# The first two key tiles of an attention stage, their penalties and the first query are loaded by another route

## The chip, the cores and the metric

The kernel runs on one core of a Trainium2 chip, as one launch. The metric is the device time of an execution in microseconds (us); of several executions the median is taken.

The core has five engines with instruction queues of their own: TensorE (PE, with its weight loads as PEld), VectorE (DVE), ScalarE (ACT), GpSimd (POOL) and SyncE (SP). In this kernel SP issues all the transfers (DMA) between the memory off the core and the core's own.

## The reference, cut to what matters

One layer of an encoder for 2048 prompt frames and 8 x 16 sample frames. A wide input projection feeds two mixers: a gated one over 128-frame chunks, and a sparse attention, in which an indexer scores all earlier keys for each query and only the best 256 take part. Their outputs are merged, projected and normed.

```python
def _sparse_attend(q, qi, wi, q_pos, k, v, kidx, k_pos, topk):
    rel = relu(einsum('bqhd,bld->bqhl', qi, kidx) * IDX_DIM ** -0.5)
    score = einsum('bqhl,bqh->bql', rel, wi) * N_IDX_HEADS ** -0.5
    score = where(chunk_mask(q_pos, k_pos), score, -inf)
    top_val, top_idx = lax.top_k(score, topk)          # 256 of up to 2048 keys
    k_sel, v_sel = k[top_idx], v[top_idx]
    logits = einsum('bqhgd,bqnhd->bqhgn', qg, k_sel) * HEAD_DIM ** -0.5
    p = softmax(where(top_val > -inf, logits, -inf))
    return einsum('bqhgn,bqnhd->bqhgd', p, v_sel)
```

## The kernel before

Rows (frames) are handled in tiles of 128: tiles 0 to 15 are the prompt, tile 16 the samples. There are three parts.

**Projections and selection.** `phase_p1` and `phase_p2` make the projections for one half of the tiles at a time. Each product is made from three matmuls of a high and a low part (`mm3`, line 175), after `split_hi` on ACT (line 181) and `split_lo` on DVE or POOL (line 184). Between these matmuls the generator `select` is woven in, once per tile, on two lanes. It makes the scores of a tile (`scores`: the indexer's query is loaded into a buffer tagged `qi`, split into `qih` and `qi`, and multiplied with the indexer's keys, lines 544 and 545), then finds the 256th largest score bit by bit, counting in turn on DVE (line 623) and on ACT (line 633). At the end it turns the scores into a penalty per key, in pieces of 512 columns: a scan on DVE (line 669) into a buffer `pre` (tag `r`, three buffers), a compare on DVE (line 674) into the buffer `pen` (one buffer), a scaling on ACT (line 675), and a store to the scratch tensor `pen_s` (line 676). All 256 first keys are chosen for tiles 0 and 1, so `select_all_of` writes their penalties at the start of the program (lines 685 to 687). The last tiles are 15 on one lane and 14 on the other.

**Attention.** `phase_b` runs over the prompt's tiles from 0 to 15. For each it loads keys, values, penalties and queries. `load_kv` transposes the key tile on PE (line 724), splits it into `kst` (ACT and DVE), and splits the values into `vst` (ACT and POOL). `attend_logits` makes the logits (lines 767 and 768), subtracts the penalties and takes the maximum on DVE (line 769), and takes the exponential on ACT (line 774). `attend_values` transposes the results (line 791) and multiplies them with the values (line 808). The samples' attention and the first merges are woven in behind.

**Merge and output**, `phase_c`.

Between the first and the second part stands `load_first` (before). It loads the key tiles 0 and 1 into buffers tagged `r`, the penalty of tile 0 into the buffer tagged `pen`, and the query of tile 0 into the indexer's buffer `qi`, which it splits into `qih` and `qi` at once. All these buffers lie in the pool `tk`, which stays open. The pool `bp` of the attention takes the room of the projections' weights.

```python
    back = weave(phase_p2(0, hT), back, 0.95)
    drain(back)
    load_first()
    wp.close()
    hp.close()
    bank.set(mm=3, tr=3, po=1, ix=1)
    bp = Pool("bp")
```

The instructions of each engine are put into a fixed order by a scheduler, which works on its own estimate of times when the program is built; each engine then works its list off from the first to the last. So a change in one place may reorder instructions in others.

## Time and profile before

| | |
|---|---|
| device time, median of 3 runs | 2202.66 us (2201.59 to 2203.26) |
| profiled execution: its own time | 2199.08 us |
| profiled execution: span from first to last instruction | 2197.3 us |
| PE busy | 2117.8 us (96%) |
| DVE busy | 1534.8 us (70%) |
| ACT busy | 1271.4 us (58%) |
| POOL busy | 588.1 us (27%) |
| mean granted TensorE clock | 0.988 of full speed |

The span is the time between the first and the last instruction of the one execution that was profiled; its own device time is 1.78 us longer. Busy time of PE is modelled from pipelined matmuls, so 96% means that it rarely stood still, not that it worked at its peak.

### The profile page before, as it was taken

The numbers are of one execution on the slowest core, as the hardware profiler recorded it, in microseconds if no ns is written. First come the engines' busy times: TensorE is split into PE (matmuls) and PEld (weight loads), VectorE is DVE, ScalarE is ACT, GpSimd is POOL, SyncE is SP. The second block draws the span as 40 slices with busy tenths as digits, with TensorE's granted clock in tenths as the row PEclk, the third lists the DMA queues.
The fourth block names the chain that finished last, engine by engine and source line by source line (L and its number), as shares of the span: only waits on it lengthen the run. The fifth ranks groups of instructions, "written<-read, shape, count | busy, mean of one in ns | idle before, by whom it ended". The sixth has DMA issues, their size and how long they took to land.

```text
span 2197.3 us, 38208 instructions
## 1 busy us (share of the span) xinstructions
PE 2117.8 (96%) x13896; PEld 2008.8 (91%) x13896; DVE 1534.8 (70%) x3926; ACT 1271.4 (58%) x2280; POOL 588.1 (27%) x693
## 2 busy tenths in 40 slices
PE   8999999999999999999999999599999999999998
PEld 7999999999999988999999999588889998987886
DVE  7128777988887847778865785587867788855443
ACT  6237666567766644556764665487766667743221
POOL 1222132222242222223252221232254433233000
PEclk9999999999999999999999999799999999999999
DMA  6234243122252323222233222454254431054342
GB/s 205 88 105 131 63 119 101 50 77 83 71 153 87 95 76 120 59 61 63 67 116 102 63 83 74 114 145 103 59 169 132 121 104 40 11 161 155 130 153 77
DMA packets 251005, 218.83 MB, mean 100 GB/s; under 512 B 46528, under 2 KB 238656, under 8 KB 250816
## 3 DMA queue, kind: packets, MB, share of 16 engines
q1 hardware_dynamic: 250816, 216.39, 33.5%
q8 instruction: 109, 1.79, 0.3%
q14 instruction: 80, 0.66, 0.1%
HBM read 152.45 MB, written 63.81 MB: 98 GB/s over the span
## 4 chain that ended last, share of the span: by engine, by line
PE 80%; DMA 6%; DVE 5%; ACT 4%; issue 2%; POOL 1%; SPq 1%; ACTq 0%; DVEq 0%; POOLq 0%
PE ps_mm L175 54%; PE ps_po L808 5%; PE ps_tr L791 5%; PE ps_mm L767 3%; PE ps_ix L544 2%; PE ps_ix L545 2%; PE ps_mm L768 2%; PE ps_ix L175 2%; DMA ws<-in_w_in_dram 2%; DMA q<-q_s 1%; POOL wl L184 1%; PE ps_mm L819 1%; DMA x<-in_x_prompt_dram 1%; DVE junk L623 1%; PE ps_tr L439 1%
## 5 line engine op out<-in xcount | busy, mean ns | idle before, releaser
L184 POOL TENSOR_TENSOR wl<-ws,wh 128x256 fp32r<-128x256 f32 (+1 forms) x376 | 300.7, 831 | 912.1 <-ACT wh L181 841.1
L175 PE MATMUL ps_mm<-wh,hh 128*128 128x256 f32 (+1 forms) x1360 | 390.4, 288 | 6.4 <-ACT hh L181 3.7
L175 PE MATMUL ps_mm<-wh,hl 128*128 128x256 f32 (+1 forms) x1360 | 392.0, 289 | 0.9 <-DVE hl L184 0.9
L175 PE MATMUL ps_mm<-wl,hh 128*128 128x256 f32 (+1 forms) x1360 | 390.0, 287 | 0.5 <-POOL wl L184 0.5
L633 ACT ACTIVATE junk<-s,bc 128x384 int8<-128x384 f32 (+14 forms) x232 | 294.0, 1267 | 154.8 <-DVE bc L639 153.0
L175 PE MATMUL ps_mm<-hh,wh 128*128 128x384 f32 (+1 forms) x1152 | 378.2, 328 | 0.0
L175 PE MATMUL ps_mm<-hl,wh 128*128 128x384 f32 (+1 forms) x1152 | 377.5, 328 | 0.0
L175 PE MATMUL ps_mm<-hh,wl 128*128 128x384 f32 (+1 forms) x1152 | 376.6, 328 | 0.0
L623 DVE TENSOR_SCALAR_CACHE_REDUCE junk<-s,bc 128x512 int8<-128x512 f32 (+14 forms) x233 | 331.0, 1422 | 5.7
L175 PEld LDWEIGHTS ps_mm<-wh,hh 128*128 128x128 f32 x1360 | 258.5, 190 | 9.8 <-ACT hh L181 4.7
L175 PEld LDWEIGHTS ps_mm<-wh,hl 128*128 128x128 f32 x1360 | 258.6, 190 | 3.1 <-DVE hl L184 1.2
L175 PEld LDWEIGHTS ps_mm<-wl,hh 128*128 128x128 f32 x1360 | 258.9, 190 | 2.4 <-POOL wl L184 0.9
L551 DVE SCALAR_TENSOR_TENSOR s<-r,wiw,s 128x384 f32<-128x384 f32 (+2 forms) x266 | 201.4, 772 | 57.3 <-ACT r L547 56.3
L175 PEld LDWEIGHTS ps_mm<-hh,wh 128*128 128x128 f32 x1152 | 216.5, 188 | 4.3 <-issue 0.7
L175 PEld LDWEIGHTS ps_mm<-hl,wh 128*128 128x128 f32 x1152 | 216.5, 188 | 3.0 <-issue 0.4
L175 PEld LDWEIGHTS ps_mm<-hh,wl 128*128 128x128 f32 x1152 | 216.4, 188 | 2.9 <-issue 0.7
L547 ACT ACTIVATE r<-ps_ix 128x512 f32<-128x512 f32 (+2 forms) x304 | 159.6, 538 | 101.0 <-PE ps_ix L545 84.2
L791 PE MATMUL ps_tr<-ident,sx 128*128 128x128 f32 x1088 | 170.8, 275 | 5.9 <-ACT sx L774 3.6
L181 ACT ACTIVATE pth<-ps_tr 128x512 fp32r<-128x512 f32 (+1 forms) x231 | 128.4, 572 | 67.8 <-PE ps_tr L791 61.9
L774 ACT ACTIVATE sx<-sx,mx 128x128 f32<-128x128 f32 (+15 forms) x128 | 153.7, 1202 | 23.9 <-DVE mx L773 23.2
L184 DVE TENSOR_TENSOR ptl<-ps_tr,pth 128x512 fp32r<-128x512 f32 (+1 forms) x231 | 150.0, 659 | 22.9 <-ACT pth L181 21.9
L808 PE MATMUL ps_po<-pth,vst 128*128 128x256 f32 x544 | 156.1, 305 | 2.1 <-ACT osb L812 1.2
(295 smaller groups left out, 4563.8 us busy)
## 6 DMA issues: line engine op xcount, KB each, us to landing
ws<-in_w_in_dram SPq DMA_DIRECT2D x88, 512.0 KB, 4.0
x<-in_x_prompt_dram SPq DMA_DIRECT2D x41, 512.0 KB, 3.6
out_dram<-x SPq DMA_DIRECT2D x17, 512.0 KB, 2.6
q<-q_s SPq DMA_DIRECT2D x32, 256.0 KB, 4.4
gb_s<-ev SPq DMA_DIRECT2D x40, 192.0 KB, 2.1
ma_s<-ev SPq DMA_DIRECT2D x40, 192.0 KB, 1.9
ma<-ma_s SPq DMA_DIRECT2D x40, 192.0 KB, 3.4
sg<-gb_s SPq DMA_DIRECT2D x40, 192.0 KB, 2.9
```

What stands on the lines that cost most here:

```text
L175: nc.tensor.matmul(out, a(k), b(k), start=(n == 0), stop=(n == 3 * nk - 1))
L181: nc.scalar.activation(dst, src, AF.Copy)
L184: (eng or nc.vector).tensor_tensor(dst, src, hi.bitcast(F32), op=OP.subtract)
L544: nc.tensor.matmul(pi[:, :n], hi[:, h, :], kist[:, c:c + n], start=True, stop=False)
L547: nc.scalar.activation(r[:, :n], pi[:, :n], AF.Relu, scale=HD ** -0.5)
L551: nc.vector.scalar_tensor_tensor(s[:, c:c + n], r[:, :n], wiw[:, t, h:h + 1], s[:, c:c + n], op0=OP.mult, op1=OP.add)
L623: nc.vector.tensor_scalar(junk[:, :L], s[:, :L], thr, 0.0, op0=op, op1=OP.add, accum_out=cnt)
L633: nc.scalar.activation(junk[:, :L], s[:, :L], AF.Sign, bias=candf, scale=-1.0, accum_out=cnt)
L767: nc.tensor.matmul(pl[:, :w], T.hi[:, h, :], kst[:, h // 2, c:c + w], start=True, stop=False)
L774: nc.scalar.activation(sx, sx, AF.Exp, bias=mx[:, 7:8], scale=HD ** -0.5, accum_out=T.rsum[:, h:h + 1])
L791: nc.tensor.transpose(tv[:, l, hh * P:(hh + 1) * P], pr[hh][:, (l0 + l) * P:(l0 + l + 1) * P], ident)
L808: nc.tensor.matmul(po, vst[:, l0 + l, n, :], pp[:, l, :], start=(l0 + l == 0 and i == 0), stop=(l0 + l == t and i == 1))
```

## The change

`load_first` is called from `select`, right after the last tile's scores are made, and no longer after the selection has drained. The two key tiles go together into one buffer tagged `qi` (4 KB per partition, the size of an indexer's query), the raw query of tile 0 into the buffer tagged `qih`. The penalties of tiles 0 and 1 get buffers of their own, `pen0` and `pen1`. The query of tile 0 is split in `attend_load`, into a buffer of the pool `bp`.

```diff
--- before.py
+++ after.py
@@ -605,6 +605,19 @@
     def signs(b, lane, L):
         return b % 2 == lane
 
+
+    unscored = set(range(2, NT))
+    first_k, first_q, begun = {}, {}, set()
+
+    def load_first():
+        k2 = tk.tile([P, 2, KV, 2, HD], F32, tag="qi", name="kk")
+        q = q_load(tk, q_s, 0, "qih")
+        for t in (0, 1):
+            first_k[t] = load_k(k2[:, t], t)
+            pen = tk.tile([P, (t + 1) * P], BF, name=f"pen{t}")
+            sync.dma_start(pen, pen_s[t][:, :(t + 1) * P])
+            first_q[t] = (q if t == 0 else None, pen)
+
     def select(t, lane):
 
         while GROUP_OF[t][0] not in asked:
@@ -613,6 +626,9 @@
         yield from take(*keys)
         s, L = yield from (scores(t) if t < NPT else scores_sample(lane))
         taken.difference_update(keys)
+        unscored.discard(t)
+        if not unscored:
+            load_first()
         junk = tk.tile([P, S], I8, tag=f"junk{lane}", name="junk")
         cand = tk.tile([P, 1], I32, tag=f"bc{lane}", name="bc")
         g = tk.tile([P, 1], I32, tag=f"bg{lane}", name="bg")
@@ -701,24 +717,15 @@
 
     KB = 1
 
-    def load_k(pool, t, tag, bufs):
-        k2 = pool.tile([P, KV, 2, HD], F32, tag=tag, name="kk", bufs=bufs)
+    def load_k(k2, t):
         for i in range(2):
             sync.dma_start(k2[:, :, i], o_k[0, 0, t * P:(t + 1) * P])
         return k2
 
-
-    first_k, first_q, begun = {}, {}, set()
-
-    def load_first():
-        for t in (0, 1):
-            first_k[t] = load_k(tk, t, "r", 3)
-        pen = tk.tile([P, 512], BF, tag="pen", name="pen")
-        sync.dma_start(pen[:, :P], pen_s[0][:, :P])
-        first_q[0] = (pen, *pair_of(tk, q_load(tk, q_s, 0, "qi"), "qih"))
-
     def load_kv(bp, kst, vst, t):
-        k2 = first_k.get(t) or load_k(bp, t, "kk", KB)
+        k2 = first_k.get(t)
+        if k2 is None:
+            k2 = load_k(bp.tile([P, KV, 2, HD], F32, tag="kk", name="kk", bufs=KB), t)
         tp = bank("tr")
         for n in range(KV):
             nc.tensor.transpose(tp[:, n * P:(n + 1) * P], k2[:, n].rearrange("p a d -> p (a d)"), ident)
@@ -742,12 +749,13 @@
     def attend_load(bp, t):
         T = Tile()
         T.t, T.L = t, (t + 1) * P
-        if t in first_q:
-            T.pen, T.hi, T.lo = first_q[t]
-        else:
+        q, T.pen = first_q.get(t, (None, None))
+        if T.pen is None:
             T.pen = bp.tile([P, S], BF, tag="pen", name="pen", bufs=2)
             sync.dma_start(T.pen[:, :T.L], pen_s[t][:, :T.L])
-            T.hi, T.lo = pair_of(bp, q_load(bp, q_s, t, "q", 2), "qh", 2)
+        if q is None:
+            q = q_load(bp, q_s, t, "q", 2)
+        T.hi, T.lo = pair_of(bp, q, "qh", 2)
         T.rsum = bp.tile([P, H], F32, tag="rsum", name="rsum", bufs=4)
         T.p = {}
         return T
@@ -1152,7 +1160,6 @@
     px[0].close()
     back = weave(phase_p2(0, hT), back, 0.95)
     drain(back)
-    load_first()
     wp.close()
     hp.close()
     bank.set(mm=3, tr=3, po=1, ix=1)
```

The order of instructions at two places follows, as the program has it. A row is: number of the row in the engine's list, line, operation, result and operands, shape; xN stands for N in a row.

ACT, from the last tile's final sign count (`junk,bl`) on, before the change (the last two evictions of the projections, `ev<-ps_mm`, stand right ahead of it); `kst` are the split keys, `vst` the split values, `qh` a split query, `pen` the penalty pieces of tile 14:

```order
1014 L659 ACTIVATE junk,bl<-s,bc 128x1920
1015 L660 ACTIVATE sq,bl<-junk 128x1920
1016 L181 ACTIVATE vst<-vf 128x4x64
1017 L675 ACTIVATE pen<-pen 128x512
1018 L181 ACTIVATE qh<-q 128x1024
1019 L181 ACTIVATE vst<-vf 128x4x64
1020 L675 ACTIVATE pen<-pen 128x512
1021 L181 ACTIVATE qh<-q 128x1024
1022 L181 ACTIVATE vst<-vf 128x4x64
1023 L675 ACTIVATE pen<-pen 128x512
1024 L181 ACTIVATE vst<-vf 128x4x64
1025 L181 ACTIVATE kst<-ps_tr 128x4x128
```

Here the first key tile's split follows the third of four penalty pieces. The same place on ACT with the change:

```order
1011 L481 ACTIVATE ev<-ps_mm 128x384 x2
1012 L675 ACTIVATE junk,bl<-s,bc 128x1920
1013 L676 ACTIVATE sq,bl<-junk 128x1920
1014 L481 ACTIVATE ev<-ps_mm 128x384
1015 L691 ACTIVATE pen<-pen 128x512 x2
1016 L181 ACTIVATE kst<-ps_tr 128x4x128
1017 L181 ACTIVATE qh<-qih 128x1024
1018 L181 ACTIVATE kst<-ps_tr 128x4x128
1019 L181 ACTIVATE vst<-vf 128x4x64
1020 L691 ACTIVATE pen<-pen 128x512
1021 L181 ACTIVATE qh<-q 128x1024
1022 L782 ACT_TABLE_LOAD
```

Both key tiles and the first query now stand behind the second piece, and the last eviction of the projections stands behind the final count instead of ahead of it. The query of tile 1 (row 1021) stands ahead of the first exponential, which follows row 1022; the query of tile 2 follows behind the fourth piece, ahead of the second four heads of tile 0.

SP, where the queries of tile 3 are loaded (`q_s_81`) beside the samples' loads (`q_s_85`, `penx`, `kc`, `vc`), before the change:

```order
491 L525 DMA q<-q_s_85 64x8x128
492 L526 DMA q<-q_s_85 64x8x128
493 L920 DMA penx<-pen_s_286 16x8x272 x8
494 L924 DMA kc<-in_cache_k_dram 128x2x256
495 L925 DMA kc<-out_dram 16x256
496 L926 DMA vc<-in_cache_v_dram 128x2x256
497 L927 DMA vc<-out_dram 16x256
498 L707 DMA kk<-out_dram 128x4x64 x2
499 L749 DMA pen<-pen_s_273 128x512
500 L525 DMA q<-q_s_81 64x8x128
501 L526 DMA q<-q_s_81 64x8x128
```

And with the change:

```order
487 L525 DMA q<-q_s_81 64x8x128
488 L525 DMA q<-q_s_85 64x8x128
489 L526 DMA q<-q_s_85 64x8x128
490 L928 DMA penx<-pen_s_286 16x8x272 x8
491 L932 DMA kc<-in_cache_k_dram 128x2x256
492 L933 DMA kc<-out_dram 16x256
493 L934 DMA vc<-in_cache_v_dram 128x2x256
494 L935 DMA vc<-out_dram 16x256
495 L526 DMA q<-q_s_81 64x8x128
496 L722 DMA kk<-out_dram 128x4x64 x2
```

The first half of tile 3's query moved ahead of the samples' loads, the second half stays behind them.

## Rows read from the trace of the kernel before

**Rows 1.** The page, part 1: busy time of each engine, its share of the span, and its instructions.

```profile
PE 2117.8 (96%) x13896; PEld 2008.8 (91%) x13896; DVE 1534.8 (70%) x3926; ACT 1271.4 (58%) x2280; POOL 588.1 (27%) x693
```

**Rows 2.** Busy time by stretches of 10 us around the end of the projections. The columns are: stretch, its length, busy time and instructions of PE, PEld, DVE, ACT and POOL, granted clock of PE, share of the DMA engines, GB/s.

```profile
1380.00:1390.00 10.00, 9.10 (x52) 8.78 (x50) 6.53 (x15) 3.45 (x5) 0.00 (x0) 1.00 0.05 20
1390.00:1400.00 10.00, 0.00 (x0) 0.00 (x0) 8.25 (x9) 3.75 (x7) 3.00 (x2) 0.61 0.76 178
1400.00:1410.00 10.00, 1.57 (x6) 1.20 (x7) 3.05 (x3) 3.48 (x6) 2.19 (x2) 0.50 0.68 160
1410.00:1420.00 10.00, 5.22 (x24) 4.63 (x25) 4.07 (x26) 5.34 (x16) 1.62 (x3) 0.50 0.42 105
...
1440.00:1450.00 10.00, 8.17 (x53) 6.69 (x54) 6.81 (x19) 8.09 (x22) 3.52 (x4) 1.00 0.65 154
```

**Rows 3.** What PE waited for between 1300 and 1500 us, longest first: total, times, longest.

```profile
PE ps_tr L724 <- DMA kk<-out_dram: 15.8, 1, 15.8
PE ps_mm L767 <- DVE mx L769: 4.0, 1, 4.0
```

**Rows 4.** Timeline of PE: start, duration, line, operands, and in brackets the idle time before and what ended it.

```profile
1404.88 1.09 PE L724 MATMUL ps_tr<-ident,kk 128*128 128x128 f32 x4 [15.78 <-DMA kk<-out_dram]
1409.52 0.47 PE L767 MATMUL ps_mm<-kst,qih 128*128 128x128 f32 x1 [3.55 <-DVE kst L184]
```

**Rows 5.** The chain of work that ended last, between 1350 and 1450 us: start, duration, piece.

```profile
1398.01 4.87 DMA q<-q_s
...
1412.07 1.69 DMA pen_s<-pen
1413.84 1.68 DMA pen<-pen_s
```

**Rows 6.** Timeline of ACT.

```profile
1387.40 1.89 ACT L659 ACTIVATE junk<-s,bc 128x1920 int8<-128x1920 f32 x1
...
1399.96 0.63 ACT L675 ACTIVATE pen<-pen 128x512 bf16<-128x512 bf16 x1 [2.22 <-DVE pen L674]
1402.96 1.06 ACT L181 ACTIVATE qh<-q 128x1024 fp32r<-128x1024 f32 x1 [2.38 <-DMA q<-q_s]
...
1408.16 0.58 ACT L181 ACTIVATE kst<-ps_tr 128x512 fp32r<-128x512 f32 x1
...
1411.54 0.51 ACT L675 ACTIVATE pen<-pen 128x384 bf16<-128x384 bf16 x1
...
1416.41 1.28 ACT L774 ACT_TABLE_LOAD   x1 [1.36 <-DVE mx L773]
1417.71 0.40 ACT L774 ACTIVATE sx<-sx,mx 128x128 f32<-128x128 f32 x1
...
1419.66 0.39 ACT L774 ACTIVATE sx<-sx,mx 128x128 f32<-128x128 f32 x1
...
1421.72 0.50 ACT L774 ACTIVATE sx<-sx,mx 128x256 f32<-128x256 f32 x1
```

**Rows 7.** Timeline of DVE.

```profile
1386.59 0.16 DVE L651 TENSOR_TENSOR bc<-bc,bg 128x1 f32<-128x1 f32 x1
...
1391.34 0.16 DVE L662 TENSOR_TENSOR bd<-bl 128x1 f32<-128x1 f32 x1 [1.59 <-ACT sq L660]
...
1404.05 1.23 DVE L184 TENSOR_TENSOR q<-q,qh 128x1024 fp32r<-128x1024 f32 x1 [4.18 <-ACT qh L181]
1405.20 1.22 DVE L674 SCALAR_TENSOR_TENSOR pen<-pre,bd,junk 128x512 bf16<-128x512 f32 x1
...
1408.77 0.69 DVE L184 TENSOR_TENSOR kst<-ps_tr,kst 64x512 fp32r<-64x512 f32 x1 [2.36 <-ACT kst L181]
...
1415.55 0.29 DVE L769 CUSTOM_DVE_ANT_0 sx<-ps_mm,pen 128x128 f32<-128x128 f32 x1 [2.25 <-DMA pen<-pen_s]
```

**Rows 8.** Timeline of DVE and SP at the place where tile 0's query is loaded and split before the change.

```profile
1276.25 1.23 DVE L184 TENSOR_TENSOR qi<-qi,qih 128x1024 fp32r<-128x1024 f32 x1 [1.41 <-ACT qih L181]
...
1271.16 0.63 SPq L526 DMA_DIRECT2D qi<-q_s  x1
1278.05 0.33 SPq L516 DMA_DIRECT2D ma_s<-ev  x1
```

**Rows 9.** Timeline of SP and of ACT: the samples' penalties, the query of tile 3 and its split.

```profile
1419.42 3.64 SPq L920 DMA_DIRECT2D penx<-pen_s  x8
...
1427.13 0.61 SPq L525 DMA_DIRECT2D q<-q_s  x1
...
1433.22 1.08 ACT L181 ACTIVATE qh<-q 128x1024 fp32r<-128x1024 f32 x1
```

**Rows 10.** Timeline of SP at the start of the program, and the transfers issued before 30 us: KB each, median us from issue to landing.

```profile
8.43 2.08 SPq L687 DMA_DIRECT2D pen_s<-pen  x1
...
16.91 0.33 SPq L687 DMA_DIRECT2D pen_s<-pen  x1
...
22.11 0.93 SPq L159 DMA_DIRECT2D ws<-in_w_in_dram  x2
...
pen_s<-pen SPq DMA_DIRECT2D x1, 64.0 KB, 1.6
pen_s<-pen SPq DMA_DIRECT2D x1, 32.0 KB, 7.6
```

**Rows 11.** Busy time in the body of the attention, columns as in Rows 2.

```profile
1460.00:1960.00 500.00, 486.63 (x3444) 452.75 (x3444) 384.74 (x1099) 343.77 (x625) 170.16 (x179) 1.00 0.34 95
```

## The prediction

> **What bounds the kernel now.** I began with the page's busy times [rows 1]: PE is busy 96% of the span, so a gain has to come from the few places where PE stands still or runs at half clock. The next view was the table of stretches around the end of the projections [rows 2]: PE is busy 9.10 of 10 us up to 1390, then 0.00, 1.57 and 5.22 us in the next three stretches, while its clock falls to 0.50. That hole is the largest of the kernel. The waits of PE name its parts [rows 3, 4]: 15.8 us for the first key tile, 3.55 us for its split on DVE, 4.0 us behind the first masked logits. PE ends its last projection at 1404.88 - 15.78 = 1389.10 and first multiplies keys with queries at 1409.52.
>
> The timelines of ACT and DVE say why the hole is so long. The last tile's selection finishes in the same time: final sign count at 1387.40 [rows 6], then scans and four penalty pieces on DVE, each scaled on ACT and stored before the next can be written. The key tiles wait for the buffers of those scans, and tile 0's penalty for the one buffer of the pieces: its load starts after the last store has landed and takes 1.68 us [rows 5], so the first masked logit is made at 1415.55 [rows 7] and the first exponential at 1417.71 [rows 6].
>
> **The change, part by part.** *The loads leave the hole.* Keys 0 and 1, query 0 and both penalties are in place long before 1389. The price is paid around 1271: four key loads more behind the query on SP. Two issues of tile 0's query take about 1.3 us there; four more of about 0.6 us are 2.5 us, and SP's next work begins only at 1278.05, when the query's second issue ended at 1271.79 [rows 8]. Those 6.3 us hide it; without them it would cost up to 2.5 us. Taken: 0.
>
> *The penalties' loads move to the start of the program.* There SP now waits, behind the store of each of the two penalties, until it has landed. The first store, issued at 8.43, lands 7.6 us later, by 16.03; the next work of SP is the second store at 16.91. That one lands 1.6 us after its issue, by 18.5, and SP's weight load comes at 22.11 [rows 10]. Both waits are covered; if the landing counts from the end of the 2.08 us issue (18.1), the second store slips by 1.5 us. Bounds 0 and 1.5, taken 0.
>
> *The split of query 0 moves into the hole.* Before, DVE paid 1.23 us for it and 1.41 us of waiting [rows 8] in the middle of the last two selections. These 2.6 us go, so the last selection ends earlier. Further, its final count no longer stands behind the last sigmoid eviction on ACT: DVE had released it at 1386.75 [rows 7], it ran at 1387.40. So DVE may go on with the scans between 0.65 us earlier than its 1391.34 (if the counting is held up by evictions it is interleaved with) and 3.2 us earlier. In the new order one more counting round stands ahead of the evictions, so I take 3.2: 1388.1.
>
> *The hole itself, walked in the new order.* From 1391.34 to the end of the second piece's scaling at 1400.59 the old path takes 9.25 us [rows 6, 7]. A query's split on DVE leaves it and an eviction enters, and the store's landing gates it anyway: 8.9 us, so 1397.0. ACT then splits key 0 (0.58) and query 0 (1.06), DVE makes the query's low part (1.23), which with the handovers gives 1400.0. PE's first three pairs follow; meanwhile DVE makes the third piece (1.22) and key 1 (0.69). The first masked logit then comes near 1401.9, which is 13.7 us earlier. On ACT the third piece is scaled by 1401.8; query 1 was issued behind the second piece's store, and with two issues and 4.87 us [rows 5] it lands at 1402.9. Its split (1.06) and the table load (1.28) make the first exponential 1405.3, 12.4 us earlier. The second four heads stand behind the split of query 2, which is issued behind the third piece's store: 1402.0 + 1.0 + 4.87 = 1407.8, and 1.06 for the split and 0.3 for a transposed result give 1409.2 against 1419.66, 10.5 us earlier. From there to tile 1's first exponential it took 2.06 us; a key-value eviction and a split more make it 2.6: 1411.8 against 1421.72. **10 us earlier at tile 1.**
>
> ACT and DVE keep their order even when a later instruction could run. The trace shows the cost: DVE stood 4.18 us for a query's split at 1404.05 with the third piece queued behind it [rows 7], though that piece's input was there. [...]
>
> *Behind the hole.* SP now issues one half of tile 3's query behind the samples' loads: 8 penalties in 3.64 us [rows 9] and six other issues stand between. From the end of tile 1's logits that makes about 7.3 us of issues, 4.87 us of landing and the split, some 14 us, where before the query went out at 1427.13 and was split at 1433.22 without a wait [rows 9]. The work ahead of it covers most; I charge 3 us. On the other side PE idled 1.83 us in 1440 to 1450 [rows 2], waiting for loads of that kind, and those start 7 to 10 us earlier: 2 back.
>
> **Sum.** 10 - 3 + 2 = 9 us. Made against the profiled execution's own 2199.08 us (span 2197.3) this is 2190.1. The median of the runs shown lies 3.58 us above that execution, so for the median I say 2202.66 - 9 = **2193.7 us**. The half clock stays about as long: PE still stands from 1390 to about 1400.
>
> The open term is the attention's order. The scheduler laid out nearly all of it anew; no trace shows the new one. PE idles 13.4 us of 500 in that body [rows 11]; an estimate from this is that a new order takes or gives up to 4 us.
>
> **The rivals.**
>
> *The selection keeps its pace.* The counting of the last tile is tied to evictions that wait for PE, so it gains only 0.65 us, and the pieces come as before. Then the third piece, made by 1406.42 [rows 7], is scaled by 1407.1, the first exponential comes at 1407.1 + 1.06 + 1.28 = 1409.4, the second heads, behind the fourth piece at 1411.54, near 1413.5: 6 us earlier, less 3, plus 2 makes 5, so 2197.7 (2195 to 2201). For it: the same ACT list carries both. Against it: DVE's 4.18 us wait is gone.
>
> *More than the sum.* The counting gains a round more (up to 2.7 us), or PE's clock does not fall: in 1400 to 1420 it was busy 6.8 us at 0.50 [rows 2], of which full clock gives 3.4 back. 9 + 3 = 12, so 2190.7; both and a lucky order: 2185. Against it: 10 us of idle remain, and in the old 15.8 us the mean clock of the first stretch had come down to 0.61 [rows 2].
>
> *The change does not do what it says.* The early buffers are there, but the first logits are held by the last selection as long as before, through its pieces on ACT and DVE: gain under 2 us, 2201 to 2203. Against it: the first key's split stands behind two pieces in the new list, not three, and the penalty's load behind none.
>
> *Slower: tile 3's query.* Its second half arrives so late that PE stops again and its clock falls a second time. The delay is at most 14 - 6 = 8 us against the old distance; a clock at 0.50 for the 15 us that it took before, from 1405 to 1420 [rows 2], would cost PE up to 7.5 us of dense work more, and the 2 us would not come back. 10 - 8 - 7.5 = -5.5, so 2208.2. [...]
>
> **How the numbers follow.** Chances: the sum 0.55 (2189.5 to 2198), the kept pace 0.20, more than the sum 0.12, no effect 0.06, slower 0.07. The range 2186.5 to 2201 leaves out about half of the "more" case's lower end, "no effect" and "slower", near 0.2 in all. A difference of 0.2% (4.4 us) is about what a measurement of this kernel can tell from none. Faster by more than it means under 2198.3: the sum, the "more" case and half of the kept pace, 0.77. The other half and "no effect" are the same: 0.16. Slower: 0.07.
>
> **What would show it.** In the changed kernel's trace PE's idle before its first key transposes should be nearly gone, and a wait of about 8 us should stand behind them, ended by ACT's or DVE's split of key or query. ACT's first exponential should come at 1405.3 (1409.4 by the kept pace), the final sign count near 1384.2 (else 1386.8), the second four heads directly behind a query's split that waited for its load, and tile 3's query split with about 3 us of wait. PE's granted clock should still touch 0.50. Up to 1389 PE's work should end at the same time within 0.5 us; if it ends later, the start or the added issues cost what I set at nothing. The prediction is wrong above all if PE's idle in the body of the attention differs from 13.4 us by more than 4.

## The result, and the profile after

The changed kernel takes 2190.39 us (median of 4 runs, 2189.17 to 2192.88) against 2202.96 us of the kernel before on the same chip (4 runs): ratio 0.9943, 95% interval 0.9926 to 0.9960, 12.6 us less. Timed again beside the kernel before (below) it gave 0.9945. The forecast was 9 us less, 2193.7 us, range 2186.5 to 2201. The profiled execution took 2190.51 us, span 2188.7 us, so the two profiled ones differ by 8.6 us; 29 executions of the kernel before on one chip ranged from 2190.6 us at a mean granted clock of 0.991 to 2204.5 us at 0.983, so one pair says less than the medians.

The page, busy time of the changed kernel:

```profile
PE 2124.0 (97%) x13896; PEld 2010.3 (92%) x13896; DVE 1533.3 (70%) x3926; ACT 1270.6 (58%) x2280; POOL 580.5 (27%) x693
```

PE's idle time, span less busy, went from 79.5 us (2197.3 - 2117.8, [rows 1]) to 64.7 us. Of these 14.8 us, 6.2 came back as longer busy time of the same 13896 matmuls. In the trace of e5, the same program run again, the busy time was 2120.3 us and the idle time 63.9.

Stretches of 10 us of the changed kernel, columns as in [rows 2]:

```profile
1380.00:1390.00 10.00, 10.00 (x61) 9.90 (x59) 6.24 (x12) 5.39 (x7) 0.00 (x0) 1.00 0.06 20
1390.00:1400.00 10.00, 3.60 (x16) 2.90 (x14) 7.51 (x19) 5.30 (x8) 0.97 (x1) 0.72 0.75 179
1400.00:1410.00 10.00, 7.81 (x43) 6.40 (x44) 8.06 (x44) 8.88 (x33) 2.95 (x3) 0.77 0.52 124
1410.00:1420.00 10.00, 8.00 (x52) 6.99 (x52) 6.48 (x27) 9.39 (x30) 5.06 (x13) 0.91 1.05 192
1420.00:1430.00 10.00, 10.00 (x59) 8.49 (x57) 7.41 (x27) 6.47 (x18) 3.66 (x4) 0.75 0.84 217
...
1440.00:1450.00 10.00, 10.00 (x74) 8.95 (x73) 8.11 (x30) 8.34 (x23) 3.86 (x4) 1.00 0.54 127
```

Where PE did 0.00, 1.57 and 5.22 us of work it now does 3.60, 7.81 and 8.00. Its clock is below full speed for less of the time, 17 us between 1386 and 1432 in place of 31 by stretches of 1 us, but PE works in that time: the full stretch from 1420 ran at 0.75.

Timeline of PE, from the last projection on:

```profile
1388.97 0.34 PE L175 MATMUL ps_mm<-ah,wl 128*128 128x384 f32 x1
1389.14 1.03 PE L731 MATMUL ps_tr<-ident,kk 128*128 128x128 f32 x8
1393.95 0.56 PE L775 MATMUL ps_mm<-kst,qh 128*128 128x128 f32 x3 [3.77 <-ACT qh L181]
1395.21 0.90 PE L776 MATMUL ps_mm<-kst,qih 128*128 128x128 f32 x3 [0.70 <-DVE qih L184]
1397.40 0.47 PE L775 MATMUL ps_mm<-kst,qh 128*128 128x128 f32 x1 [1.29 <-DVE mx L777]
...
1401.08 1.25 PE L799 MATMUL ps_tr<-ident,sx 128*128 128x128 f32 x3 [1.71 <-ACT sx L782]
```

The 15.78 us in front of the first key transposes [rows 4] are gone; behind them PE waits 3.77 + 0.70 + 1.29 + 1.71 = 7.5 us for splits, masks and exponentials. Timeline of ACT:

```profile
1380.86 0.49 ACT L481 ACTIVATE ev<-ps_mm 128x384 f32<-128x384 f32 x1 [5.83 <-PE ps_mm L175]
1381.25 1.89 ACT L675 ACTIVATE junk<-s,bc 128x1920 int8<-128x1920 f32 x1
...
1387.21 0.49 ACT L481 ACTIVATE ev<-ps_mm 128x384 f32<-128x384 f32 x1 [2.06 <-PE ps_mm L175]
...
1391.84 0.63 ACT L691 ACTIVATE pen<-pen 128x512 bf16<-128x512 bf16 x1 [2.73 <-DVE pen L690]
1392.37 0.58 ACT L181 ACTIVATE kst<-ps_tr 128x512 fp32r<-128x512 f32 x1
...
1398.16 1.06 ACT L181 ACTIVATE qh<-q 128x1024 fp32r<-128x1024 f32 x1 [1.16 <-DMA q<-q_s]
...
1400.53 0.40 ACT L782 ACTIVATE sx<-sx,mx 128x128 f32<-128x128 f32 x1
...
1405.51 0.39 ACT L782 ACTIVATE sx<-sx,mx 128x128 f32<-128x128 f32 x1
...
1407.62 0.49 ACT L782 ACTIVATE sx<-sx,mx 128x256 f32<-128x256 f32 x1
...
1423.78 1.06 ACT L181 ACTIVATE qh<-q 128x1024 fp32r<-128x1024 f32 x1 [1.76 <-DMA q<-q_s]
```

The final sign count stands at 1381.25, 6.15 us ahead of the 1387.40 of [rows 6]; the first exponential is 17.2 us earlier, the second four heads 14.2, tile 1's first exponential 14.1. Timeline of DVE: the selection's end, the second and third penalty piece, the first masked logit.

```profile
1385.19 0.16 DVE L678 TENSOR_TENSOR bd<-bl 128x1 f32<-128x1 f32 x1 [1.59 <-ACT sq L676]
...
1391.06 0.74 DVE L690 SCALAR_TENSOR_TENSOR pen<-pre,bd,junk 128x512 bf16<-128x512 f32 x1
...
1395.07 1.22 DVE L690 SCALAR_TENSOR_TENSOR pen<-pre,bd,junk 128x512 bf16<-128x512 f32 x1
...
1397.05 0.29 DVE L777 CUSTOM_DVE_ANT_0 sx<-ps_mm,pen 128x128 f32<-128x128 f32 x1
```

Timeline of SP at the start of the program and where keys and query 0 are loaded:

```profile
8.73 2.08 SPq L703 DMA_DIRECT2D pen_s<-pen  x1
...
16.27 0.33 SPq L618 DMA_DIRECT2D pen<-pen_s  x1
17.21 0.33 SPq L703 DMA_DIRECT2D pen_s<-pen  x1
...
18.85 0.32 SPq L618 DMA_DIRECT2D pen<-pen_s  x1
22.40 0.93 SPq L159 DMA_DIRECT2D ws<-in_w_in_dram  x2
...
1272.21 2.61 SPq L722 DMA_DIRECT2D kk<-out_dram  x4
1277.91 0.33 SPq L516 DMA_DIRECT2D ma_s<-ev  x1
```

### The profile page after: what moved, and what is told of

It is laid out like the page before. It is cut to its first block, busy times and chain, and to the rows that moved or that the text cites. A ratio compares the mean times of both kernels' runs of the same rounds, so it can differ in the third digit from the quotient of the medians.

```text
span 2188.7 us, 38200 instructions
## 1 busy us (share of the span) xinstructions
PE 2124.0 (97%) x13896; PEld 2010.3 (92%) x13896; DVE 1533.3 (70%) x3926; ACT 1270.6 (58%) x2280; POOL 580.5 (27%) x693
## 4 chain that ended last, share of the span: by engine, by line
PE 78%; DMA 7%; DVE 5%; ACT 5%; issue 3%; POOL 2%; SPq 1%; ACTq 0%; POOLq 0%; DVEq 0%
PE ps_mm L175 51%; PE ps_po L816 5%; PE ps_tr L799 5%; PE ps_mm L775 3%; PE ps_mm L776 2%; PE ps_ix L544 2%; PE ps_ix L175 2%; PE ps_ix L545 2%; DMA ws<-in_w_in_dram 2%; POOL wl L184 1%; PE ps_mm L827 1%; DVE junk L639 1%; ACT junk L649 1%; DMA bl<-bt_s 1%; ACT wh L181 1%
## 5 line engine op out<-in xcount | busy, mean ns | idle before, releaser
L175 PEld LDWEIGHTS ps_mm<-wh,hh 128*128 128x128 f32 x1360 | 258.3, 190 | 10.3 <-ACT hh L181 4.8
L184 DVE TENSOR_TENSOR ptl<-ps_tr,pth 128x512 fp32r<-128x512 f32 (+1 forms) x231 | 149.6, 660 | 29.1 <-ACT pth L181 27.3
L782 ACT ACTIVATE sx<-sx,mx 128x128 f32<-128x128 f32 (+15 forms) x128 | 153.7, 1203 | 19.0 <-DVE mx L781 18.6
```

Source lines behind the costliest of these rows:

```text
L175: nc.tensor.matmul(out, a(k), b(k), start=(n == 0), stop=(n == 3 * nk - 1))
L184: (eng or nc.vector).tensor_tensor(dst, src, hi.bitcast(F32), op=OP.subtract)
L782: nc.scalar.activation(sx, sx, AF.Exp, bias=mx[:, 7:8], scale=HD ** -0.5, accum_out=T.rsum[:, h:h + 1])
```

## How the runs are read

Every run is measured from the end of its own last projection on PE, since that end lay between 1384.9 and 1389.8 us in the traces. Two stretches of the table by stretches give PE's idle time: the 32 us behind that end ("hole"), and the 608 us behind those ("body"). Of the kernel before, then of the changed one:

```profile
1389.10:1421.10 32.00, 7.89 (x34) 6.93 (x35) 16.91 (x44) 14.55 (x36) 7.91 (x8) 0.55 0.60 142
1421.10:2029.10 608.00, 584.35 (x3983) 538.30 (x3982) 457.95 (x1292) 401.49 (x770) 218.13 (x238) 0.99 0.39 109
```

```profile
1389.10:1421.10 32.00, 21.42 (x120) 17.66 (x118) 23.98 (x92) 23.58 (x70) 10.05 (x16) 0.80 0.75 164
1421.10:2029.10 608.00, 586.31 (x3966) 537.93 (x3965) 449.85 (x1247) 390.85 (x734) 215.93 (x232) 0.99 0.38 110
```

That is 32 - 7.89 = 24.1 us of idle in the hole before and 10.6 after, 23.7 and 21.7 in the body. The stretch of [rows 11] in the changed kernel, for the order's term of the prediction:

```profile
1460.00:1960.00 500.00, 483.84 (x3385) 448.73 (x3383) 378.30 (x1069) 336.13 (x608) 170.44 (x181) 0.99 0.34 97
```

All runs measured in the hole and the body, with the first exponential counted from the last projection, and the ratio of times to the kernel before:

| kernel | first exp. | hole idle | body idle | ratio (95% interval) |
|---|---|---|---|---|
| before | 28.6 | 24.1 | 23.7 | 1 |
| changed | 11.4 | 10.6 | 21.7 | 0.9943 (0.9926 to 0.9960) |
| e5 changed again | 11.5 | 11.3 | 24.1 | 0.9945 (0.9932 to 0.9958) |
| e1 split in hole | 20.5 | 16.8 | 29.1 | 1.0021 (1.0008 to 1.0033) |
| e2 rooms only | 22.7 | 18.6 | 33.0 | 1.0056 (1.0036 to 1.0075) |
| e3 keys, no rooms | 21.5 | 17.7 | 29.9 | 1.0034 (1.0022 to 1.0045) |
| e4 samples at 3 | 11.3 | 12.3 | 25.0 | 0.9984 (0.9973 to 0.9995) |
| e6 pieces on POOL | 11.4 | 9.4 | 19.8 | 0.9940 (0.9928 to 0.9952) |
| e7 POOL, in place | 12.2 | 10.7 | 27.5 | 0.9974 (0.9961 to 0.9986) |
| e8 changed, rate 0.16 | 12.8 | 11.6 | 27.0 | 0.9969 (0.9958 to 0.9981) |
| e9 pieces 2 to 4 late | 13.8 | 12.8 | 25.3 | 0.9958 (0.9944 to 0.9971) |
| e10 all pieces late | 13.4 | 14.5 | 27.1 | 0.9986 (0.9975 to 0.9996) |
| e11 before, rate 0.30 | 28.3 | 23.8 | 29.3 | 1.0034 (1.0020 to 1.0049) |
| e12 exps ahead | 7.6 | 10.3 | 29.0 | 0.9964 (0.9953 to 0.9975) |

The ratios alone are the verdict on the time; idle times are from one trace each. e1 to e4 ran on one chip, where the kernel before took 2195.6 us (29 runs), 3.5 to 7.4 us less than in the other comparisons. Why it did better there stays open; set against those others, the four ratios would be some 0.002 to 0.003 lower (3.5 and 7.4 of 2200). So these four are judged by the idle times and against each other.

## The experiments

**The parts (e1, e2, e3).** e1 leaves keys and penalty as before and only moves the split of query 0:

```diff
 # before, load_first
-        first_q[0] = (pen, *pair_of(tk, q_load(tk, q_s, 0, "qi"), "qih"))
+        first_q[0] = (pen, q_load(tk, q_s, 0, "qi"))
 # attend_load
-            T.pen, T.hi, T.lo = first_q[t]
+            T.pen, q = first_q[t]
+            T.hi, T.lo = pair_of(bp, q, "qh", 2)
```

> The kernel before with one part of the change: query 0 is still loaded early and still into the indexer's query buffer, but its split is written to the attention's own buffer and so stands in the hole; keys and penalty as before. Theory A (three chains: the counting, the keys' buffers, the penalty's room; the latest sets the first exponential): the final sign count comes at 1381.3 as in the changed kernel (before 1387.4), the penalty pieces near 1388.5, 1392, 1397 and 1402, and the keys, which wait for the scans' buffers, and tile 0's penalty, which waits for the fourth piece's store, come some 6 to 9 us earlier than before: first exponential near 1409 to 1411 (before 1417.7, changed 1400.5), ratio near 0.997 to 0.998. Theory B (the counting alone makes the gain): first exponential within 2 us of 1400.5, ratio as the changed kernel's 0.994. Theory C (the earlier count has another cause, such as the keys' early loads): final count stays at 1387.4, ratio 1.000.

e2 takes the kernel before and gives only the penalties rooms, that is, buffers of their own (cut to the loads):

```diff
 # before, load_first
+        load_pens()
 # the loads of the keys, as before
-        pen = tk.tile([P, 512], BF, tag="pen", name="pen")
-        sync.dma_start(pen[:, :P], pen_s[0][:, :P])
 # load_pens
+        for t in (0, 1):
+            early_pen[t] = tk.tile([P, (t + 1) * P], BF, name=f"pen{t}")
+            sync.dma_start(early_pen[t], pen_s[t][:, :(t + 1) * P])
```

> The kernel before with the other part alone: the penalties of tiles 0 and 1 lie in rooms of their own and are loaded early; keys and query 0 as before. Theory A: the final sign count stays at 1387.4; the first masked logit comes near 1408 to 1409 in place of 1415.55, since only the keys hold it; the first exponential stands behind the fourth piece on ACT (before 1411.54) and the table load, near 1412.8, some 5 us earlier; ratio 0.998. Theory B (the counting alone): no gain, ratio 1.000, first exponential within 1 us of 1417.7 less the penalty's load.

e3 is the changed kernel without the rooms, so it has two of the three parts, the moved split and the early keys:

```diff
 # changed, load_first
-            pen = tk.tile([P, (t + 1) * P], BF, name=f"pen{t}")
-            sync.dma_start(pen, pen_s[t][:, :(t + 1) * P])
-            first_q[t] = (q if t == 0 else None, pen)
+            first_q[t] = (q if t == 0 else None, None)
 # behind drain(back): the old load of pen_s[0] into the tag "pen"
```

> The changed kernel without the rooms: keys 0 and 1 and query 0 early, the penalty of tile 0 loaded behind the last piece into the pieces' buffer, that of tile 1 as for any later tile. Theory A: final count 1381.3, first key transposes right behind the projections at 1389.1, but the first masked logit waits for the fourth piece's store and the load behind it: near 1405 to 1407, first exponential near 1408 (changed 1400.5, before 1417.7); ratio near 0.997. Theory B (the counting alone): as the changed kernel, first exponential within 2 us of 1400.5 and ratio 0.994.

Where the early count comes from is told by ACT's timeline. The selection of a tile counts in turn on DVE and ACT, and tile 14, the last one, is 1920 keys wide. The kernel before: the split of query 0, the first of tile 14's counts on ACT, and the last two ahead of the final one:

```profile
1275.16 1.06 ACT L181 ACTIVATE qih<-qi 128x1024 fp32r<-128x1024 f32 x1 [3.24 <-DMA qi<-q_s]
...
1288.18 1.88 ACT L633 ACTIVATE junk<-s,bc 128x1920 int8<-128x1920 f32 x1
...
1371.02 1.90 ACT L633 ACTIVATE junk<-s,bc 128x1920 int8<-128x1920 f32 x1 [2.49 <-DVE bc L639]
...
1377.33 1.90 ACT L633 ACTIVATE junk<-s,bc 128x1920 int8<-128x1920 f32 x1 [2.50 <-DVE bc L639]
```

The changed kernel, the first and the last of these counts; then the first of e1 and of e2:

```profile
1280.81 1.90 ACT L649 ACTIVATE junk<-s,bc 128x1920 int8<-128x1920 f32 x1 [0.17 <-DVE bc L655]
...
1371.22 1.90 ACT L649 ACTIVATE junk<-s,bc 128x1920 int8<-128x1920 f32 x1 [2.49 <-DVE bc L655]
```

```profile
1276.54 1.90 ACT L633 ACTIVATE junk<-s,bc 128x1920 int8<-128x1920 f32 x1 [0.18 <-DVE bc L639]
```

```profile
1285.76 1.88 ACT L633 ACTIVATE junk<-s,bc 128x1920 int8<-128x1920 f32 x1
```

Each of the four programs has 15 of these counts and then the final one (L659, in the changed kernel L675). Counted from the last projection, the first stands at -100.9 us before and -100.7 in e2, at -108.3 in the changed kernel and -108.5 in e1; the final one at -1.7 in the first two, at -7.9 and -8.0 in the others. The split's leaving alone does it: with it goes ACT's wait of 3.24 us for the query, the counting begins 7.4 us earlier, and at its end it is one round ahead. A round takes 6.3 us there (1371.02 to 1377.33). The final count stands right behind an eviction in both kernels, so its place there is not the cause. Theory C falls, and so does theory B, since the first exponential of e1 is not near that of the changed kernel.

Theory A holds for the first exponential: e1, e2 and e3 bring 6 to 8 us (20.5, 22.7, 21.5 against 28.6), all parts together 17.2. The chain that is left holds each of them: in e1 the keys come 6.2 us behind the last projection, and tile 0's penalty then holds the first masked logit on DVE for 4.75 us; in e2 PE waits 15.5 us for the keys; in e3, where the keys are early, the penalty holds it for 5.1 us, and so the keys bring nothing beyond e1's split. The split and the rooms without the early keys were not run. The hole's idle falls by 7.3, 5.5 and 6.4 us, together by 13. But not one of the three is faster as a whole, which neither theory had: the body's idle rises from 23.7 to 29.1, 33.0 and 29.9.

**Is that the order alone? (e8, e11, and e5 as the measure.)** e8 and e11 change one number of the weaving:

```diff
-    BACK_RATE = 0.15
+    BACK_RATE = 0.16   # e8, in the changed kernel; e11: 0.30, in the kernel before
```

> The changed kernel itself, unaltered, timed in more runs beside the kernel before. In the first comparison (4 runs each) it was 12.6 us faster; the two profiled executions differ by 8.6 us of span, and PE's idle and half-clock time behind the projections by 66.4 - 54.0 = 12.4 us; the variant with the samples at tile 3, alike up to tile 2, was only 2.8 us faster than the kernel before over 12 runs. Theory G (before was timed on few runs at its slow end; the gain is 3 to 6 us): ratio 0.997 to 0.9985. Theory H (the gain is the trace's 8 to 12 us, and the samples' later begin cost the difference): ratio 0.9945 to 0.9965.

> The changed kernel with one number of the weaving changed, the share of samples' and merging work laid beside the attention, 0.15 to 0.16. No buffer, load or wait is touched and the hole is the same, row by row, up to the middle of tile 3; only the order of the attention's instructions from there differs. Theory K (an order of its own moves the time by several us): PE's idle and half-clock time behind the first 72 us (changed 35.2 us, the three parts alone 32 to 41) differs by 2 to 8 us from the changed kernel's, and the time with it, either way. Rival L (an order costs next to nothing, and what the parts lost has other causes): within 1.5 us.

> The kernel before with the share of the woven work at 0.30 in place of 0.15: as for the changed kernel at 0.16, no buffer, load or wait is touched, the hole is the same, and only the order of the attention's instructions from tile 4 on differs. Theory K (the order alone is worth several us, and the old kernel's order was a good one): PE's idle behind the first 72 us rises from 20.8 us to 23 to 28, as in the three parts run alone (23.2, 28.4, 26.1); time 2 to 8 us longer, ratio 1.001 to 1.004. Rival L: within 1.5 us of the kernel before.

The body of e8, and of e11:

```profile
1421.10:2029.10 608.00, 581.03 (x3950) 535.05 (x3950) 447.15 (x1245) 389.60 (x733) 214.64 (x231) 0.99 0.38 109
```

```profile
1421.10:2029.10 608.00, 578.69 (x3902) 532.47 (x3901) 450.76 (x1271) 398.32 (x762) 214.85 (x236) 0.97 0.38 106
```

Theory H holds: 11.9 us faster again (2187.17 against 2199.11 us). And theory K: with the hole nearly as it was (10.6 to 11.6, as query 1 landed later in that trace; 24.1 to 23.8), an order that differs from the middle of tile 3 or tile 4 on cost 2192.49 - 2187.17 = 5.3 us in the changed kernel and 2209.12 - 2200.98 = 8.1 us in the kernel before, with 27.0 and 29.3 us of idle in the body. Two traces of one program differ there by 2.4 us (21.7 and 24.1). Before and after both have a good order; most others made here have not. So what e1 to e3 lost is of the size that an order alone costs; that it was the order and nothing else isn't shown for them.

**Tile 3's query (e4).** `while 2 not in begun` in `attend_sample` becomes `while 3 not in begun`.

> The changed kernel with one number changed: the samples' attention may begin when tile 3 has begun, not tile 2, so that both halves of tile 3's query are issued ahead of the samples' eight penalties. Theory D (tile 3's query makes the second half-clock stretch of the changed kernel, 6.8 us near 1418 to 1425): the split of tile 3's query on ACT comes some 8 us earlier and without the 1.76 us wait, the second stretch at 0.50 is gone or shorter, PE idle in 1410 to 1440 falls from 2.8 us to about 1; 3 us of the span come back, ratio near 0.9930. Rival E (that stretch comes from the thin work of tiles 0 to 2 at 1400 to 1420, and tile 3's query is covered): the second stretch stays, ratio 0.994 to 0.995. Rival F: the samples' loads, now later, stop PE somewhere in 1430 to 1470 and cost what is gained.

The split of tile 3's query came at 1414.78 with 0.80 us of wait (1423.78 and 1.76 in the changed kernel), so that part of theory D was so, and the second stretch at half clock was shorter (0.90 and 0.93 in 1410 to 1430, against 0.91 and 0.75). But PE's idle from 1410 to 1440 rose from 2.8 to 5.9 us, 2.2 of them one wait for DVE; the hole kept 12.3 us of idle, not less than 10.6 or 11.3, and the ratio is no better. Nor is that stretch tied to the query: e5, the same program as the changed kernel with the same wait (1.58 us), kept 1.00 there and fell later, behind a wait of 2.4 us for ACT (0.83 in 1426 to 1436). D falls. In the changed kernel none of PE's waits from 1380 to 1440 is ended by that split, so its wait is covered there.

**What bounds the rest of the hole (e6, e7, e9, e10, e12).** e6 scales all pieces made after the last scores, those of tiles 15 and 14, with `nc.gpsimd.tensor_scalar(pen[:, :m], pen[:, :m], 0.0, BIG, op0=OP.max, op1=OP.mult)`; e7 also writes each of these pieces into its scan's buffer (`pen = pre.bitcast(BF)[:, :512]`).

> The changed kernel; the pieces of the last tile's penalty are scaled on POOL instead of ACT, so that no piece stands ahead of the keys' split on ACT. Theory I (the first key's split waits behind two pieces in ACT's fixed order, 3.2 us from the end of the projections to it): the split of key 0 comes 1.3 us behind the last projection, the first masked logit 2 us earlier counted from there (changed 7.9), the first exponential 1 to 2 us earlier (changed 11.4 behind the last projection, held then by query 1's load); idle in the first 16 us falls from 7.5 to about 5.5. Rival J (DVE is the one that holds it, through the piece that waits there for the store of the one before): under 0.5 us. For the whole time either may be lost in the attention's new order, which moved the three parts run alone by 5 to 10 us: ratio to the changed kernel 0.996 to 1.004.

> As the one before (last tile's pieces scaled on POOL), and each piece is written into the buffer of its own scan (three of them) instead of the one piece buffer, so that DVE never waits for a store. Theory I and J together: the four pieces follow each other in about 2 us each instead of 3.4, 4.5 and 6.3, all stored by 10 us behind the last projection; query 1's load is issued earlier, first exponential 2 to 3 us earlier than in the changed kernel (11.4 behind the last projection). If the first masked logit gains no more than with POOL alone, DVE's wait for the stores was covered (rival to J). Whole time: 0.996 to 1.004 of the changed kernel by the order.

In e6 (last projection 1389.8) ACT split the first key 0.6 us behind the last projection (3.2 in the changed kernel), and DVE stood with the key's low part queued behind the second piece:

```profile
1390.42 0.60 ACT L181 ACTIVATE kst<-ps_tr 128x512 fp32r<-128x512 f32 x1 [2.07 <-PE ps_tr L734]
```

```profile
1394.31 0.75 DVE L690 SCALAR_TENSOR_TENSOR pen<-pre,bd,junk 128x512 bf16<-128x512 f32 x1 [2.36 <-DMA pen_s<-pen]
```

So rival J holds: the wait moved from ACT to DVE. e7 took that wait away too, but all four pieces of tile 14 stood ahead of the splits on DVE, and POOL needed 9.46 us for them (ACT takes 0.63 us for one): the first exponential came at 12.2, nothing gained.

e9 and e10 emit tile 14's pieces behind the first logits, the second piece (e10: the first) ordered on DVE behind the low part of query 0's split:

```diff
+            if t == 14 and c == 512:    # e10: c == 0
+                issue_behind(made, first_lo[0])
```

> The changed kernel; the last tile's second, third and fourth penalty pieces are made on DVE only behind the low part of query 0's split, so that on ACT the first key's split follows one piece, not two, and on SP query 1's load no longer stands behind the second piece's store. Moving the pieces to POOL had brought the split on ACT 2.6 us forward, but not the first exponential, because DVE then waited for the first store with the key's low part queued behind the second piece. Theory M (the fixed order of ACT and DVE holds the splits, and only taking the pieces off both helps): key 0's split on ACT some 1.3 us behind the last projection (changed 3.2), its low part on DVE about 2 us behind it (changed 3.9), first masked logit near 5 us (changed 7.9), first exponential 8.5 to 10 (changed 11.4); idle in the first 16 us 5 to 6 in place of 7.4. Rival N (query 1's load holds the first exponential whatever the keys do): first exponential stays at 11 to 11.5. Whole time 0.993 to 1.003 of the changed kernel, the spread being the new order's.

> As the one before, with all four pieces behind the low part of query 0's split. Theory M: key 0's split as early as there; first masked logit up to 1 us earlier than there, since DVE has no piece at all ahead; first exponential 8 to 9.5 us behind the last projection. Rival N: 11 to 11.5 as in the changed kernel. The pieces end later (the last one some 25 us behind the last projection), which nothing waits for before tile 14. Whole time 0.993 to 1.003 of the changed kernel.

The first masked logit came 5.4 and 4.9 us behind the last projection (7.9 in the changed kernel), as theory M says. The first exponential came at 13.8 and 13.4 us, later than in the changed kernel and than either theory had it. Rival N is right in that query 1's split stands ahead of it on ACT and waits for its load (e9); behind that split stand the second piece and tile 1's value split, which waits 1.19 us more:

```profile
1398.88 1.06 ACT L181 ACTIVATE qh<-q 128x1024 fp32r<-128x1024 f32 x1 [4.31 <-DMA q<-q_s]
```

e12 adds to e9 that tile 1's value and query split are ordered on ACT behind tile 0's first four exponentials (`issue_behind(ins, last_exp[0])`).

> As the run with pieces two to four behind query 0, and besides tile 1's query split and value split stand on ACT behind tile 0's first four exponentials. There the first masked logit had come 5.4 us behind the last projection (changed 7.9), but the first exponential only at 13.8 (changed 11.4), with ACT idle for 4.3 us on query 1's load and 1.2 us on the values'. Theory N (ACT's fixed order, with query 1's split ahead of the exponentials, holds them): first exponential now at 6.5 to 7.5, behind the second piece and the table load; idle in the first 16 us falls from 10.0 us to 5 to 7, in the first 32 us from 12.8 to 8 to 10. Rival O (the hole is bounded by query 1's load itself, since tile 0 alone gives PE little): first exponential early as said, but idle in the first 32 us stays within 1.5 us of the changed kernel's 10.6 to 11.4. Whole time: 0.991 to 1.002 of the changed kernel, its order being new again.

The exponential came at 7.6 (N: 6.5 to 7.5), and the hole stayed at 10.3 us of idle, the number of rival O. PE's timeline of e12, and ACT's:

```profile
1398.42 0.65 PE L817 MATMUL ps_tr<-ident,sx 128*128 128x128 f32 x2
1402.78 0.58 PE L792 MATMUL ps_mm<-kst,qh 128*128 128x256 f32 x1 [3.70 <-ACT qh L181]
```

```profile
1401.36 0.42 ACT L181 ACTIVATE vst<-vf 128x256 fp32r<-128x256 f32 x1 [2.99 <-DMA vf<-out_dram]
1401.68 1.04 ACT L181 ACTIVATE qh<-q 128x1024 fp32r<-128x1024 f32 x1
```

Tile 0's logits are soon done, and PE then waits 3.70 us for query 1's split. But O's cause, query 1's load, isn't shown: its two halves were issued at 1392.08 and 1392.74 and landed at most 5.7 us later, so by 1398.5, and the split ran at 1401.68. Ahead of it on ACT stood tile 1's value split, whose load landed only at 1401.3. So some 3 of the 3.70 us are again a fixed order, one that e12 made. The query's split ahead of the values' was not run. Query 1's load itself goes out 2.9 us behind the last projection (1.7 in e10); on SP it stands behind the store of the last eviction (1391.19) and the load of tile 0's values (1391.60). Whether a buffer outside `bp`, the pool that takes the room the projections give up, would bring it forward wasn't tried.

No variant beats the changed kernel by more than its interval; e6 equals it.

With the call of `load_first` put back to its old place and the new buffers kept, the built program has the same instructions in the same order on all five engines. The buffers decide where the loads stand, not the place of the call.

## Why the prediction was right, step by step

- **Early loads hidden: right.** Four key issues took 2.61 us (said: 2.5), and SP's next work came at 1277.91 (1278.05 before, [rows 8]).
- **Waits at the start: right.** The second store came 0.3 us later than in [rows 10], as did the first; the projections ended at the same time as before, 1389.1. That agreement is luck and proves little: in e5, the same program, they ended at 1384.9.
- **The selection's end: the mis-sized term.** Said 3.2 us, measured 6.15 (1391.34 to 1385.19). I priced the removed split by its 2.6 us on DVE, held it to 3.2, and put "a round more" (up to 2.7 us) into a rival. The trace of the kernel before had more: the split also held ACT for 3.24 us of wait, and the counting moved by a whole round, 6.3 us at its end. It began 7.4 us earlier and ended one round earlier. The "more than the sum" rival (2190.7 us) named this mechanism, and its 3.2 + 2.7 = 5.9 us is near the measured 6.15.
- **The hole's walk: right in its chain, about 4.5 us late.** First masked logit 1397.05 (said 1401.9), first exponential 1400.53 (1405.3), second four heads 1405.51 (1409.2), tile 1 1407.62 (1411.8). Some 3 us are the selection's; from its end to the second piece's scaling it took 7.3 us, not 8.9; 0.9 of these 1.6 us are the first two pieces on DVE, 0.73 and 0.74 us in place of 1.15 and 1.21. The links were those named: two pieces ahead of the key's split, query 1's split ahead of the exponential. ACT kept its order there: the key's transposes had ended by 1390.17, but its split ran at 1392.37, behind the second piece, for which ACT stood 2.73 us. PE's wait behind the transposes was 7.5 us (said: about 8).
- **Behind the hole: right in kind.** Tile 3's query waited 1.76 us on ACT (charged 3), and none of PE's waits was ended by its split; the 1.83 us of idle at 1440 to 1450 are gone. Over the 40 us behind the hole PE's idle fell from 2.9 to 1.5 us (2 was said to come back).
- **The order's ±4: right for this order, too narrow as a bound.** In the prediction's own stretch, 1460 to 1960, PE idled 16.2 us in place of 13.4 [rows 11]; over the body it is -2.0 us in one trace and +0.4 in the other, all within the 4. Eight of the other eleven programs, e8 and e11 among them, had 27 us or more of idle in the body. Such an order would have taken 5 to 8 us of the gain, and the time would have been 2195 to 2198 us: the forecast held this term at ±4 without a row that showed it. Nothing in it could tell which order the scheduler would make, so that this was a good one is luck.
- **The clock: wrong in part.** It touched 0.50 (1395 to 1404 and 1419 to 1425), but not "about as long": 0.61, 0.50, 0.50 [rows 2] became 0.72, 0.77, 0.91 and 0.75, now over busy stretches. PE's busy time behind the last projection rose from 752.1 us to 759.0, and to 755.5 in e5. An estimate from stretches of 1 us: of it PE worked 20.7 us at half clock before, 26.6 in the changed kernel and 18.3 in e5. At 0.50 four key transposes took 1.09 us [rows 4], at 1.00 eight took 1.03. So the clock explains some 3 us in the one trace and nothing in the other; where the rest of the longer busy time comes from stays open.

From the last projection to the end the kernel before took 808.2 us, the changed one 799.6 and 799.3 in its two traces, so 8.6 and 8.9 us less. The sum, 10 - 3 + 2, came near that by errors that partly cancelled: the hole gave 13 us, not 10, and PE was then busy 6.9 and 3.4 us longer, a term that the sum did not have. The medians moved further, by 12.6 and 11.9 us: the profiled execution of the kernel before was 3.9 us under its median, and I carried a gain worked out on it over to the median. Where those 3 to 4 us lie, the one trace of the kernel before can't show.

## What to carry to other kernels

A chain that takes turns on two engines, woven between other work, can move by a whole round: here an operation of 1 us in its way, with its wait of 3 us, was worth one round, 6 us, at the chain's end. So price what you remove by its wait on every engine it stood on, and by a round of the chain, not by its own duration. Where a scheduler orders the program, a change reshuffles everything behind it; measure what an order alone is worth with an edit that touches nothing else (here 5 to 8 us), before a part is called useless or useful. And three chains that end together must be shortened together. Before you name a wait's cause, look at what stands ahead of the waiting operation in its queue: it may be another operation's wait.

## What the runs showed of the hardware

The same 128x512 penalty piece on DVE took 0.73 to 0.75 us with POOL idle and 1.15 to 1.22 us beside POOL's split of the values: in the changed kernel 0.74 at 1391.06, 1.22 at 1395.07 while POOL ran from 1394.77 to 1395.74. That split, 0.73 us in the median of 16, took 1.46 to 1.51 us beside the three such pieces of the kernel before. POOL of the changed kernel, then POOL and DVE of the kernel before:

```profile
1394.77 0.97 POOL L184 TENSOR_TENSOR vst<-vf,vst 128x256 fp32r<-128x256 f32 x1 [34.74 <-ACT vst L181]
```

```profile
1392.98 1.49 POOL L184 TENSOR_TENSOR vst<-vf,vst 128x256 fp32r<-128x256 f32 x1 [32.94 <-ACT vst L181]
```

```profile
1393.87 1.15 DVE L674 SCALAR_TENSOR_TENSOR pen<-pre,bd,junk 128x512 bf16<-128x512 f32 x1
```

Each of these slow DVE pieces ended 0.55 or 0.56 us behind the POOL operation beside it; why, no run shows. In e7 a piece at 1387.35 took 0.75 us while POOL scaled others. Scaling a 128x512 piece took 1.92 to 2.82 us on POOL against 0.63 on ACT.
